# A running log-sum-exp: loads issued by GpSimd, stores by SyncE

## The chip, the cores and the metric

The kernel runs on one core of one Trainium2 chip. The metric is the device time of one execution in microseconds (us). Three runs of the kernel before gave 1262.72, 1262.72 and 1263.03 us, median 1262.72 us.

The core's engines are called PE (matrix products), ACT (ScalarE, exponentials and logarithms), DVE (VectorE), POOL (GpSimd) and SP (SyncE, which only issues transfers here). Transfers between DRAM and the on-chip memory are carried out by 16 DMA engines, whichever engine issues them.

## The reference

```python
B, S, D = (4, 4096, 4128)
out[:, 0, :] = x[:, 0, :].copy()
for t in range(1, S):
    mx = np.maximum(out[:, t - 1, :], x[:, t, :])
    out[:, t, :] = mx + np.log(np.exp(out[:, t - 1, :] - mx) + np.exp(x[:, t, :] - mx))
```

For each of the 4 batches and 4128 columns, row t of the output is the logarithm of the sum of the exponentials of rows 0 to t of the input. Input and output are fp32, 270.5 MB each.

## The kernel before

The work is cut into 44 *steps*. A step is a run of 384 rows of one batch (r = 3 rows for each of the 128 partitions), or 256 rows (r = 2) for one step in each batch: the first of batch 0, the last of the others. Partition p holds the r consecutive rows that begin at row p*r of the step, so its part of a transfer is one contiguous run of r x 4128 x 4 bytes: 49,536 bytes for r = 3, 33,024 for r = 2. A transfer of a step is 6192 KB or 4128 KB.

A step's tile `xt` is loaded once (line 127), worked on in place, and stored once from the same tile (line 130). The pool `xpool` has four such tiles, so step s uses the buffer of step s-4.

A step is worked in four *chunks* of columns: three of 1024 and a last one of 1056, whose last 32 columns (the tail) go through a small tile `qt`. For each chunk:

- `exp` (line 142): ACT takes the exponential of all r rows at once and writes fp16 over the tile's own memory.
- `head` (lines 92 and 96): PE sums over partitions with triangular fp16 matrices into a PSUM tile `pt`, and adds the carry of the step before, through the matrix `pick`.
- `stage(j)` for row j: ACT takes the logarithm of `pt` into the tile (line 175); PE then adds the next row through the identity. After the last row `keep` (lines 106 and 107) lets DVE save the last sums as the carry, split into two fp16 parts.

The order of the work is written out by hand in the loop of lines 205 to 218, and each engine carries out its instructions in that order. In turn g, ACT does the logarithms of chunks g-2, g-1 and g, then the exponential of chunk g+2. So the last logarithms of a step come after the first exponentials of the next step, and ACT stands still in the middle of a step's end when the next step's load has not landed.

Transfers: the first four loads are issued ahead of everything (lines 199 and 200). After a step's last logarithm its store is issued (line 211) and right behind it the load of the step three further on (line 213), into the buffer whose store was issued a step earlier. All loads and stores are issued by SP, in one queue. An instruction in a queue waits for its own conditions and holds up those behind it: a store waits for ACT's last logarithm of its step, a load for the landing of the store that last used its buffer.

POOL builds four constant matrices at the start (`_constants`, lines 18 to 46) and does nothing more; its last two instructions there are the two selects that make `pick`.

Of the kernel before, what the change touches and what calls it, by code (L numbers as in the profile page):

```python
# [49 lines left out]
def kernel(  # L50
# [11 lines left out]
    nc = tc.nc  # L62
# [49 lines left out]
    class Step:  # L112
# [10 lines left out]
        def load(self):  # L123
            full = xpool.tile([P, R, D], FP32, name="xt")
            self.xt = full[:, :self.r, :]
            self.half = self.xt.bitcast(FP16)
            nc.sync.dma_start(out=self.xt, in_=self.dram(x))  # L127

        def store(self):
            nc.sync.dma_start(out=self.dram(out), in_=self.xt)  # L130
# [118 lines left out]
```

## Time and profile before

| | |
|---|---|
| median of 3 runs | 1262.72 us |
| span of the profiled execution, first to last instruction | 1261.0 us |
| median of the runs less that span | 1.7 us |
| ACT busy | 947.0 us (75%) |
| PE busy | 690.7 us (55%) |
| DVE busy | 451.4 us (36%) |
| POOL busy | 2.2 us, 13 instructions |
| moved by DMA | 541.46 MB, 429 GB/s over the span |
| read from and written to HBM | 270.53 MB each |
| load of 6192 KB, issue to landing, median | 42.2 us |
| store of 6192 KB, issue to landing, median | 28.1 us |
| granted TensorE clock, mean | 0.779 |

The page gives no other time of the profiled execution than its span. The span begins with the first instruction and ends with the last; the median of the runs holds 1.7 us more.

"Busy" is the time in which an engine works on an instruction; issuing a transfer and waiting are not counted. A line "A <- B: total, times, longest" says that A sat idle until B released it. "SPq" is SP's queue of transfers. A transfer's line in the timeline gives the time at which it was issued and how long the issuing took, not the moving of the bytes. The trace also holds a record of each DMA packet, with start, duration and size.

### The profile page before, as it was taken

What the parts mean: (1) busy time and instruction counts of PE and PEld (TensorE: products, weight loads), DVE (VectorE), ACT (ScalarE), POOL (GpSimd) and SP (SyncE); (2) the same over time, 40 slices, a digit from 0 to 9 for tenths busy, and PEclk for the clock granted to TensorE, in tenths of its full rate; (3) what the DMA queues carried; (4) which work ended last, traced back from release to release, by engine and by line L of the source; (5) the groups of instructions that cost most, each with busy time, mean ns of one, the idle gap of its engine ahead of it and who ended that gap; (6) DMA issues with size and microseconds to landing.
All of it is one profiled execution on the core that took longest, in us unless ns stands there. A gap on an engine that the chain in (4) does not pass through costs nothing.

```text
span 1261.0 us, 6165 instructions
## 1 busy us (share of the span) xinstructions
PE 690.7 (55%) x2268; PEld 236.3 (19%) x2268; DVE 451.4 (36%) x445; ACT 947.0 (75%) x733; POOL 2.2 (0%) x13
## 2 busy tenths in 40 slices
PE   3666545565565555555346655555534755555562
PEld 1222111121121111111112221211211211111120
DVE  2443333333333333334424333333442433333344
ACT  5997777777777777778569777777866977777784
POOL 0000000000000000000000000000000000000000
PEclk9987787877777777878778777777777778787776
DMA  9999999999999999999999999999999999999998
GB/s 411 411 443 428 432 429 437 431 431 434 437 429 431 431 439 431 434 427 434 436 431 433 434 431 438 430 434 432 435 431 433 437 430 434 433 434 431 433 420 348
DMA packets 12702, 541.46 MB, mean 429 GB/s; under 512 B 1408, under 2 KB 1408, under 8 KB 1408
## 3 DMA queue, kind: packets, MB, share of 16 engines
q1 hardware_dynamic: 12672, 541.07, 99.4%
q8 instruction: 18, 0.29, 0.1%
q14 instruction: 12, 0.10, 0.0%
HBM read 270.53 MB, written 270.53 MB: 429 GB/s over the span
## 4 chain that ended last, share of the span: by engine, by line
DMA 72%; ACT 19%; PE 5%; issue 2%; DVE 1%; SPq 0%; ACTq 0%
DMA xt<-in_x_dram 67%; ACT xt L142 10%; ACT xt L175 9%; DMA out_dram<-xt 5%; PE pt L96 3%; PE pt L92 2%; DVE carry L106 0%; DVE carry L107 0%; ACT xt L180 0%; SPq L130 0%; ACTq L244 0%; SPq L127 0%; ACTq L142 0%; PE qt L92 0%
## 5 line engine op out<-in xcount | busy, mean ns | idle before, releaser
L142 ACT ACTIVATE xt<-xt 128x3072 f16<-128x3072 f32 (+3 forms) x176 | 478.2, 2717 | 247.9 <-DMA xt<-in_x_dram 247.8
L175 ACT ACTIVATE xt<-pt 128x1024 f32<-128x1024 f32 x512 | 487.3, 1029 | 2.5 <-PE pt L96 0.7
L106 DVE CAST carry<-pt 32x1024 f16<-32x1024 f32 x176 | 216.5, 1230 | 760.9 <-ACT xt L175 760.7
L92 PE MATMUL pt<-xt,ident 128*128 128x512 f16 x176 | 76.6, 435 | 493.7 <-ACT xt L175 493.7
L96 PE MATMUL pt<-xt,ident 128*128 128x512 f16 x496 | 203.7, 477 | 35.4 <-ACT xt L175 34.7
L107 DVE TENSOR_TENSOR carry<-pt,carry 32x1024 f16<-32x1024 f32 x176 | 215.8, 1226 | 6.1
L96 PE MATMUL pt<-xt,excl 128*128 128x512 f16 x496 | 187.6, 496 | 0.0
L96 PEld LDWEIGHTS <-ident 128*128 128x128 f16 x496 | 51.0, 103 | 655.0 <-issue 641.3
L92 PE MATMUL pt<-xt,incl 128*128 128x512 f16 x176 | 92.2, 524 | 23.5 <-ACT xt L142 15.1
L92 PE MATMUL pt<-xt,excl 128*128 128x512 f16 x176 | 93.4, 531 | 0.0
L96 PE MATMUL pt<-xt,incl 128*128 128x512 f16 x176 | 92.9, 528 | 0.0
L96 PEld LDWEIGHTS <-excl 128*128 128x128 f16 x536 | 66.6, 124 | 104.1 <-issue 79.5
L92 PE MATMUL pt<-carry,pick 128*128 128x512 f16 x160 | 72.0, 450 | 0.0
L96 PE MATMUL pt<-carry,pick 128*128 128x512 f16 x160 | 68.5, 428 | 0.0
L180 ACT ACTIVATE xt<-qt 128x96 f32<-128x96 f32 (+1 forms) x44 | 10.9, 248 | 46.3 <-PE pt L96 46.3
L92 PEld LDWEIGHTS <-incl 128*128 128x128 f16 x220 | 22.6, 103 | 118.0 <-DVE carry L107 95.3
L92 PEld LDWEIGHTS <-excl 128*128 128x128 f16 x220 | 26.8, 122 | 36.8 <-issue 27.9
L96 PEld LDWEIGHTS <-incl 128*128 128x128 f16 x260 | 27.8, 115 | 10.9 <-issue 4.8
L92 PEld LDWEIGHTS <-pick 128*128 128x128 f16 x200 | 22.9, 114 | 30.4 <-issue 20.4
L96 PEld LDWEIGHTS <-pick 128*128 128x128 f16 x160 | 18.4, 115 | 28.6 <-issue 17.2
L92 PEld LDWEIGHTS <-ident 128*128 128x128 f16 x176 | 19.2, 109 | 22.7 <-issue 12.8
L106 DVE CAST carry_t<-qt 32x32 f16<-32x32 f32 x44 | 8.7, 197 | 26.0 <-ACT xt L180 25.8
(21 smaller groups left out, 56.5 us busy)
## 6 DMA issues: line engine op xcount, KB each, us to landing
xt<-in_x_dram SPq DMA_DIRECT2D x40, 6192.0 KB, 42.2
out_dram<-xt SPq DMA_DIRECT2D x40, 6192.0 KB, 28.1
xt<-in_x_dram SPq DMA_DIRECT2D x4, 4128.0 KB, 37.3
out_dram<-xt SPq DMA_DIRECT2D x4, 4128.0 KB, 29.6
```

What stands on the lines that cost most here:

```text
L92: nc.tensor.matmul(pt, lhsT=w, rhs=rhs, start=start, stop=stop, skip_group_check=True)
L96: pe.add_instruction(mybir.InstMatmult(name=nc.get_next_instruction_name(), ins=[pe.lower_ap(rhs), pe.lower_ap(w, for_matmul_weights=True) ...
L106: nc.vector.tensor_copy(cr[HI:HI + 32, :], pt[HI:HI + 32])
L107: nc.vector.tensor_tensor(out=cr[LO:LO + 32, :], in0=pt[HI:HI + 32], in1=cr[HI:HI + 32, :], op=mybir.AluOpType.subtract,)
L142: nc.scalar.activation(self.t.half[:, :, 2 * c0:2 * c0 + w], self.t.xt[:, :, c0:c0 + w], ACT.Exp,)
L175: nc.scalar.activation(t.xt[:, j, c * CH:(c + 1) * CH], pt, ACT.Ln)
L180: nc.scalar.activation(t.xt[:, :, t0:D], self.qt, ACT.Ln)
```

## The change

The loads are issued by GpSimd, whose DMA descriptors are written by software; the stores stay on SP's hardware queue. One line differs:

```diff
         def load(self):
             full = xpool.tile([P, R, D], FP32, name="xt")
             self.xt = full[:, :self.r, :]
             self.half = self.xt.bitcast(FP16)
-            nc.sync.dma_start(out=self.xt, in_=self.dram(x))
+            nc.gpsimd.dma_start(out=self.xt, in_=self.dram(x))
 
         def store(self):
             nc.sync.dma_start(out=self.dram(out), in_=self.xt)
```

In the built program, the order of instructions on PE, DVE and ACT is the same as before. SP's list holds the 44 stores alone. POOL's list holds the 44 loads in the same order: the first stands between the two selects of `pick`, the others behind the second. Each of the 40 later loads carries its waits, the landing of a store among them, onto POOL.

## The prediction

> **What bounds the kernel now.** I read the page's DMA part first, because the engine part leaves it open: ACT, the busiest engine, works 75% of the span.
>
> ```profile
> DMA  9999999999999999999999999999999999999998
> q1 hardware_dynamic: 12672, 541.07, 99.4%
> DMA 72%; ACT 19%; PE 5%; issue 2%; DVE 1%; SPq 0%; ACTq 0%
> ```
>
> The first line is the share of the 16 DMA engines that is busy, in 40 slices; the second says that one queue (SP's) carried 12,672 packets and 541.07 MB and kept the engines busy for 99.4% of the span; the third is the chain that ended last. The kernel is bound by the DMA engines, not by a wait: 0.994 x 1261.0 = 1253.4 us of the span they are at work. Next, the table of stretches (columns: length, busy time of PE, PEld, DVE, ACT, POOL, granted clock, DMA share, GB/s):
>
> ```profile
> 0.00:15.00 15.00, 0.00 (x0) 0.10 (x1) 1.96 (x5) 3.15 (x2) 2.16 (x13) 1.00 0.94 387
> 100.00:1180.00 1080.00, 598.06 (x1953) 203.96 (x1953) 383.26 (x376) 815.74 (x631) 0.00 (x0) 0.77 1.00 433
> 1215.00:1230.00 15.00, 8.70 (x35) 3.12 (x34) 5.84 (x7) 12.53 (x12) 0.00 (x0) 0.89 0.93 401
> 1230.00:1245.00 15.00, 8.68 (x32) 2.92 (x31) 12.59 (x13) 12.79 (x13) 0.00 (x0) 0.89 0.79 338
> 1245.00:1261.00 16.00, 0.00 (x0) 0.00 (x0) 2.00 (x2) 0.00 (x0) 0.00 (x0) 0.51 0.84 363
> ```
>
> From 100 to 1180 us the share is 1.00 and the rate 433 GB/s; all the idle DMA time lies at the edges: 0.06 x 15 = 0.9 us at the start, and 1.05 + 3.15 + 2.56 = 6.8 us in the last 46 us. So anything that only moves waits in the middle is worth nothing; a change must alter the cost of a byte, the start, or the tail.
>
> The cost of a byte is in the trace's packet records: a packet of 33,024 B (a partition's part of a two-row step) takes 1222 ns, one of 49,536 B (three rows) 1829 ns, both medians, loads and stores alike. The difference, 607 ns for 16,512 B, is 27.2 GB/s for one engine, and leaves 1222 - 607 x 2 = 8 ns fixed for a packet. Only 3.9 us per engine is lost in packets that took longer than these medians.
>
> Last, who holds up the queue (waits of SP, then of ACT: total, times, longest):
>
> ```profile
> SPq L130 <- ACT xt L175: 1174.4, 44, 30.0
> SPq L127 <- DMA out_dram<-xt: 18.4, 5, 4.9
> ```
> ```profile
> ACT xt L142 <- DMA xt<-in_x_dram: 247.8, 42, 11.8
> ```
>
> SP stands nearly always at a store, waiting for the last logarithm. A load behind it found its buffer's earlier store already landed in all but 5 of its waits (18.4 us in all).
>
> **The change, part by part.** It removes 44 loads from SP's queue, adds 44 to POOL's, and so splits one ring of descriptors on each DMA engine into two, loads and stores. By the listing of both programs PE, DVE and ACT keep their order. Each load after the fourth now waits on POOL for its buffer's store to land; behind that wait stand only later loads, and who waits for those is ACT's first exponential.
>
> 1. *A load no longer stands behind the next store's wait for ACT.* Here is one period:
>
> ```profile
> 1153.19 0.33 SPq L130 DMA_DIRECT2D out_dram<-xt  x1
> 1153.61 0.38 SPq L127 DMA_DIRECT2D xt<-in_x_dram  x1
> 1182.54 0.33 SPq L130 DMA_DIRECT2D out_dram<-xt  x1
> 1182.97 0.38 SPq L127 DMA_DIRECT2D xt<-in_x_dram  x1
> ```
>
> The load follows the store by 0.43 us, once in 29.36 us, which is the engines' time for one load and one store: 2 x 8 x 1.829 = 29.3. The earlier store that frees the buffer takes 28.1 us (median, page) from issue to landing, so it lands about 1.2 us before. In two rings with equal turns a store of 14.6 us takes twice that, 29.3: the load is released where it was, within about 1 us. Value: 0. What hides an error is the work queued: a load lands 42.2 us after its issue, of which the store ahead and its own transfer are 29.3, so about 13 us of the load before is still running. With that cover gone ACT would wait longer, and as the engines would then run dry, each us would be one us of time.
>
> 2. *SP's issue time.* 44 x 0.383 us leaves SP; the engines had work meanwhile. 0.
>
> 3. *POOL's side.* Generating descriptors in software is not in this trace. Below: the 0.383 us that SP needs. Above: a row of unlike work, the 1.5 us of SP's longest load issue. Either is far below the 13 us of cover, so 0 in steady state. The Trainium skill speaks against the change here ("SBUF — State Buffer", Door 1's box on the "DVE blocks DMA" trap): a VectorE instruction in a two-port mode locks GpSimd out of the port it writes descriptors through. The trace has DVE at 451.4 us, its casts 1230 ns for 1024 elements a lane, from PSUM; I read 1.2 ns an element as no such mode. Were the rule to apply, a load would start at most one cast, 1.2 us, late each time, behind the 13 us: the sum would be the same.
>
> 4. *The start.* This is not hidden: the engines are saturated from the first packet on, so what the first load loses, the end loses. SP issues it at 0.80 us, and the packet records show its first data at 1.8 us. On POOL it comes between the two selects for `pick`:
>
> ```profile
> 1.95 0.29 POOL L35 TENSOR_SCALAR_AFFINE_SELECT ident<-ident 128x128 f16<-128x128 f16 x1
> 2.20 0.65 POOL L35 TENSOR_SCALAR_AFFINE_SELECT pick<-pick 128x128 f16<-128x128 f16 x2
> ```
>
> The first of the last pair ends at about 2.5: 1.7 us later than SP's 0.80. From issue to first data SP needs 1.0 us; on POOL the extra lies between 0 and three times SP's longest issue (dispatch, generation, start), 4.5 us. I take 1.3, as the usual rows (0.4 and 1.0) are nearer the low end. Together +3.0, from +1.7 to +6.2.
>
> 5. *The tail.* Before, the last load is issued at 1182.97 and lands at 1220.64; the last stores but one and two are issued at 1211.96 and 1234.00. By the packet records the engines ran dry before the store of 1234.00 for 3.4 us each in the mean. With two rings: at 1183 the load before the last has half its time, 7.3 us, left and lands 14.6 later, at 1197.6 (now 1196.1); the store issued with it lands at 1212; the last load (9.8 us) has had 7.3 by then and shares with the next store until 1217; that store's other 12.1 us end at 1229. ACT, from a landing at 1197.6, reaches the next store at about 1234 as before (it waited only 1.3 us for the last load). The hole is then 1229 to 1235, 6 us instead of 3.4: +2.6. The other end is that the hole closes: -3.4. I take +1.
>
> 6. *Cost of a load's bytes by software descriptors and of turns between rings.* 5,632 load packets on 16 engines are 352 for each. Below: the 3.9 us of stretched packets vanish if the other ring fills such gaps. Above: a load's 49,536 B are cut into their three rows, 2 x 8 ns x 352 = 5.6 us; into 4,096 B pieces, 12 x 8 ns x 352 = 33.8 us. I take 0: both kinds carry the same access shape, 128x12384, and that row is the nearest. The Trainium skill has a rule against it ("DMA: Bandwidth & Descriptors", Measured): its table for loads issued from GpSimd gives 79.0 us for 16 MB, which is 212 GB/s by its own two columns, though it prints 425 GB/s beside them; by the times, an estimate from that page, the loads alone would need 1274 us and the program far more than now, by the printed rate hardly more than now. No run here shows a software load yet; I side with the printed rate, since the row of 1829 ns stands for 433.
>
> **Sum:** span 1261.0 + 3.0 (start) + 0 (steady) + 1 (tail) + 0 (bytes) = 1265.0. The runs shown have a median of 1262.72, 1.7 above the profiled span; the forecast is 1265.0 + 1.7 = **1266.7 us**.
>
> **Rivals.** A measurement of this kernel tells about 0.2% from no change, 2.5 us: 1260.2 to 1265.2.
>
> - *Only the start and tail move* (forecast, 0.55): 1261 to 1272. For it: share 1.00 over 1080 us. About three fifths of it lies above 1265.2.
> - *The two rings fill the holes* (not slower; 0.18): a ring with loads gives an engine work while the other is empty or stretched, so the 3.4 us of the tail and the 3.9 us of long packets go, and the start keeps its least, +2: 1262.7 - 7.3 + 2 = 1257.4. It decides as soon as the start costs less than what is recovered. Against it: the hole at the tail is ACT's last step, which no ring shortens.
> - *Software descriptors or turns between rings cost* (slower by more; 0.25): 12.6 us, 1%, needs 36 ns for a load packet; pieces of 4 KB give 1262.7 + 33.8 + 3 = 1299.5, 50 ns give 1262.7 + 17.6 + 2.7 = 1283. It decides from 8 ns, where 2.8 us pass the bound. Against it: 8 ns fixed is all a packet costs now.
> - *The change is no change* (0.02): the loads wait for the same landings as before, POOL starts as early as SP; 1262.7.
>
> **The numbers.** Faster: the second case, 0.18. Same: two fifths of the first and the last, 0.22 + 0.02, less a little that I give to the slower side: 0.23. Slower: 0.59. The range goes from the second case's 1257.4 to the third's 1283 at 50 ns; I leave out some 0.05 below and 0.12 above.
>
> **What would show it.** Two dynamic queues with half the packets each, of the same sizes and durations (step 6); first load on POOL near 2.5 us, its data near 5 (step 4); loads still issued about every 29.3 us, stores landing in about 29 (step 1); 433 GB/s in the middle; the tail's share near that of now (step 5). I am wrong if the middle's rate falls below 430 or load packets multiply (third rival), if the last 46 us lose less than 4 us (second), or if POOL's issue takes over 13 us.

## The result, and the profile after

The changed kernel takes 1279.87 us, the median of four runs (1270.31 to 1284.79), against 1262.85 us for the kernel before (1262.72 to 1263.03). The ratio is 1.0125, 95% interval 1.0106 to 1.0144: slower by 1.25%. (In ratios, an execution over 1.5% above the quickest of its kernel is left out as slow; below there is one such, of 1287.70 us.) Not only the level has changed: the runs of before lie within 0.3 us, those after within 14.5 us. The profiled execution is the quickest of the four, 1270.31 us with a span of 1268.6 us. It shows where 7.6 us went; a second trace, further down, shows a slower execution, of 1276.32 us. No execution as slow as the median was traced.

The page's DMA queues and chain of the changed kernel:

```profile
DMA packets 12703, 541.47 MB, mean 427 GB/s; under 512 B 1408, under 2 KB 1408, under 8 KB 1408
q0 software_dynamic: 6336, 270.54, 49.7%
q1 hardware_dynamic: 6336, 270.54, 49.5%
...
DMA 65%; ACT 27%; issue 4%; PE 3%; DVE 0%; POOL 0%; ACTq 0%; POOLq 0%
```

Two queues carry half each, with as many packets as before, and by the packet records the software queue's packets have the same sizes and the same medians, 1222 and 1829 ns. So the packets of the software queue are not smaller, and a packet's usual cost is the same. The engines are still busy for 99.2% of a longer span. The stretches of the changed kernel (same columns as in the prediction: the last two are DMA share and GB/s):

```profile
0.00:15.00 15.00, 0.00 (x0) 0.00 (x0) 1.97 (x5) 1.28 (x1) 4.38 (x17) 1.00 0.81 328
100.00:550.00 450.00, 248.88 (x801) 84.80 (x801) 153.23 (x150) 335.14 (x257) 7.95 (x15) 0.75 1.00 433
580.00:620.00 40.00, 26.98 (x88) 9.31 (x88) 22.24 (x22) 36.59 (x32) 0.53 (x1) 0.80 0.96 399
880.00:920.00 40.00, 22.99 (x81) 8.03 (x80) 14.56 (x14) 30.94 (x25) 1.06 (x2) 0.79 1.01 426
```

The same two short stretches of the kernel before:

```profile
580.00:620.00 40.00, 22.67 (x82) 7.81 (x81) 18.92 (x18) 29.43 (x25) 0.00 (x0) 0.84 1.01 435
880.00:920.00 40.00, 23.05 (x80) 7.90 (x79) 15.52 (x16) 34.24 (x29) 0.00 (x0) 0.80 1.00 433
```

The start has less of its first 15 us (share 0.81 against 0.94). From 100 to 550 us nothing is lost. Two new losses appear, and they look different: from 580 to 620 us the share falls to 0.96, engines stand idle; from 880 to 920 us the share is 1.01 and the rate still only 426 GB/s: engines are "busy", but with packets that take longer. (A packet's whole time counts in the stretch in which it starts, so a share can pass 1.00.) Both stretches lie around a two-row step.

The loads' waits on POOL, the page's issue lines for the three-row steps, and the issue times around the first hole, of loads and then of a store, in the changed kernel:

```profile
POOL xt L127 <- ACT xt L175: 742.8, 26, 29.0
POOL xt L127 <- DMA out_dram<-xt: 347.9, 11, 65.1
```
```profile
xt<-in_x_dram POOLq DMA_DIRECT2D x40, 6192.0 KB, 36.2
out_dram<-xt SPq DMA_DIRECT2D x40, 6192.0 KB, 35.6
```
```profile
567.49 0.53 POOL L127 DMA_DIRECT2D xt<-in_x_dram  x1 [29.26 <-ACT xt L142]
592.82 0.53 POOL L127 DMA_DIRECT2D xt<-in_x_dram  x1 [24.80 <-ACT xt L175]
624.31 0.53 POOL L127 DMA_DIRECT2D xt<-in_x_dram  x1 [30.96 <-DMA out_dram<-xt]
```
```profile
592.52 0.33 SPq L130 DMA_DIRECT2D out_dram<-xt  x1
```

Each load now waits on POOL, and what it waits for is a landing: where the profile names ACT it infers, since by the listing the conditions are the same each time, the landing and earlier work of ACT that the store itself had waited for. The median load lands 36.2 us after its issue (42.2 before), the median store 35.6 (28.1 before). With equal turns a transfer of 14.64 us needs 29.3 us, so 6.9 us of a load's time and 6.3 of a store's are left for what comes ahead of its own packets. One ring had 13 us of work ahead of a load; each of the two has about half that time in hand. (That 6.9 and 6.3 add up to 13 proves nothing: the two rings run side by side, so these are waits and not amounts of work.) As the store that frees a buffer lands later, the load is issued later too: 6.8 us behind the store that was issued last (median of 40), where it was 0.4 us. At the hole, SP issued a store at 592.52, POOL a load at 592.82. By the packet records most engines had ended all earlier work of both rings by 591 to 593 and got the new store's first packet at 593.4, the new load's at 598 to 600, 5 to 7 us after its issue; the store's packet just before the load's took 2.4 to 3.0 us instead of 1.83 on nearly all engines. So there is first an idle time, as both rings are empty, and then a stretched packet. The fine stretches show the idle time, first in the profiled execution, then, at the same place, in the second trace of the same kernel:

```profile
590.00:592.00 2.00, 2.00 (x6) 0.76 (x5) 0.00 (x0) 2.00 (x2) 0.00 (x0) 0.50 0.73 314
```
```profile
592.00:594.00 2.00, 2.00 (x7) 0.75 (x5) 0.00 (x0) 2.00 (x2) 0.00 (x0) 0.51 0.16 66
```

**A ledger.** The packet records allow a full account of a span: the time to the first data, 1249.6 us per engine for all packets at their medians (1248.8 for 10,240 packets at 1829 ns and 1024 at 1222 ns, divided by 16, and 0.8 for 1408 semaphore packets at 9 ns), what packets took beyond these medians ("stretched"), idle engine time between first and last packet ("gaps"), and what follows the last packet. The last column counts first packets of a transfer that started on an engine whose ring for that kind of transfer had had nothing for over 2 us; two-ring kernels only.

| us per engine | span | first data | stretched | gaps | after the last | ring dry at start |
|---|---|---|---|---|---|---|
| before | 1261.0 | 1.8 | 4.4 | 3.9 | 1.3 | - |
| changed | 1268.6 | 3.9 | 8.0 | 5.6 | 1.5 | 26% |
| changed, second trace | 1274.6 | 4.0 | 10.8 | 8.8 | 1.5 | 49% |

The 7.6 us of the profiled execution are 2.1 (start) + 3.6 (stretched) + 1.7 (gaps, of which 0.3 in the last 60 us) + 0.2. In the second trace, of 1276.32 us, the start is the same, and stretched packets and gaps take 6.4 and 4.9 us. So in these two traces the start is fixed, and the difference between them lies in the other two.

### The profile page after: what moved, and what is told of

It is laid out like the page before. It is cut to its first block, busy times and chain, and to the rows that moved or that the text cites. A ratio compares the mean times of both kernels' runs of the same rounds, so it can differ in the third digit from the quotient of the medians.

```text
span 1268.6 us, 6172 instructions
## 1 busy us (share of the span) xinstructions
PE 688.0 (54%) x2268; PEld 236.8 (19%) x2268; DVE 451.4 (36%) x445; ACT 947.3 (75%) x733; POOL 25.6 (2%) x57
## 2 busy tenths in 40 slices
DMA packets 12703, 541.47 MB, mean 427 GB/s; under 512 B 1408, under 2 KB 1408, under 8 KB 1408
## 4 chain that ended last, share of the span: by engine, by line
DMA 65%; ACT 27%; issue 4%; PE 3%; DVE 0%; POOL 0%; ACTq 0%; POOLq 0%
DMA xt<-in_x_dram 51%; DMA out_dram<-xt 14%; ACT xt L142 14%; ACT xt L175 13%; PE pt L96 2%; PE pt L92 1%; ACT xt L180 0%; DVE carry L106 0%; DVE carry L107 0%; ACTq L244 0%; POOL xt L127 0%; POOL pick L35 0%; POOL ident L35 0%; POOL excl L25 0%; POOLq L127 0%
## 5 line engine op out<-in xcount | busy, mean ns | idle before, releaser
L92 PE MATMUL pt<-xt,incl 128*128 128x512 f16 x176 | 91.7, 521 | 26.3 <-ACT xt L142 17.4
L127 POOL DMA_DIRECT2D xt<-in_x_dram x44 | 23.5, 533 | 1173.0 <-ACT xt L175 742.8
L92 PEld LDWEIGHTS <-pick 128*128 128x128 f16 x200 | 22.6, 113 | 29.7 <-issue 19.3
## 6 DMA issues: line engine op xcount, KB each, us to landing
xt<-in_x_dram POOLq DMA_DIRECT2D x40, 6192.0 KB, 36.2
out_dram<-xt SPq DMA_DIRECT2D x40, 6192.0 KB, 35.6
```

What stands on the lines that cost most here:

```text
L92: nc.tensor.matmul(pt, lhsT=w, rhs=rhs, start=start, stop=stop, skip_group_check=True)
L127: nc.gpsimd.dma_start(out=self.xt, in_=self.dram(x))
```

## The experiments

Times are medians with lowest and highest and the number of runs; "before" beside them was 1262.78, 1262.91 and 1262.88 us in the three groups, within 0.6 us of its median each time.

### First group: software descriptors, or two rings?

Theory A blamed two rings, theory B the software descriptors.

**Two hardware rings.** ACT issues the stores.

```diff
-            nc.sync.dma_start(out=self.dram(out), in_=self.xt)
+            nc.scalar.dma_start(out=self.dram(out), in_=self.xt)
```

> Loads stay on SP's hardware queue, the stores are issued by ACT's hardware queue: two rings, but no software descriptors. Theory A (two rings whose loads and stores run at the same time stretch packets, wherever the descriptors come from): 1270 to 1285 us, with a spread of some us between executions, as in the changed kernel, less its late start of 2.5 us. Theory B (the software descriptors cost): 1262 to 1266 us with the small spread of before, the difference being ACT's issue of 44 stores.

Measured: 1265.30 us (1264.83 to 1277.23, 8 runs), ratio 1.0047 (1.0018 to 1.0077). Neither theory has it right. Five runs lie at 1264.8 to 1265.3, one at 1267.6, two at 1276.4 and 1277.2: two rings alone can cost 14 us, without a single software descriptor, but mostly don't. The trace is of a quick execution (1265.01 us); the slow ones have none.

**One software ring.** GpSimd issues loads and stores, in the order of before.

```diff
-            nc.sync.dma_start(out=self.xt, in_=self.dram(x))
+            nc.gpsimd.dma_start(out=self.xt, in_=self.dram(x))
-            nc.sync.dma_start(out=self.dram(out), in_=self.xt)
+            nc.gpsimd.dma_start(out=self.dram(out), in_=self.xt)
```

> Loads and stores are all issued by GpSimd, in the order that SP had before: software descriptors, but one ring. Theory A: the start is 2.5 us later, all else as before: 1264 to 1267 us, small spread. Theory B: at least as slow as the changed kernel, 1275 us or more, as twice as many descriptors are written by software.

Measured: 1268.34 us (1268.24 to 1268.39, 4 runs), ratio 1.0043 (1.0028 to 1.0058). Theory B, with its 1275 us or more, falls. The page and its issue lines:

```profile
q0 software_dynamic: 12672, 541.07, 99.0%
...
xt<-in_x_dram POOLq DMA_DIRECT2D x40, 6192.0 KB, 41.8
out_dram<-xt POOLq DMA_DIRECT2D x40, 6192.0 KB, 27.8
```

With all 88 transfers in software the times to landing are those of before, and so is the spread. In the ledger the 5.5 us of span are 2.2 at the start, 3.8 after the last packet (5.1 against 1.3), +0.5 stretched, -0.9 gaps: nothing in the body. The end, which puts the time above theory A's 1267 us, was not expected: POOL's longest drain at the end took 19.4 us, while the last packet ended at 1261.4.

**Loads on SP, stores on GpSimd.**

```diff
-            nc.sync.dma_start(out=self.dram(out), in_=self.xt)
+            nc.gpsimd.dma_start(out=self.dram(out), in_=self.xt)
```

> Loads on SP, stores on GpSimd: two rings, the software one carrying the stores, and the start as early as before. Theory A: 1268 to 1283 us, the changed kernel's time less 2.5 us of start, with its spread. Theory B, with a cost for each software descriptor: about the same as the changed kernel, 1270 to 1283 us; with a cost that lies in the reading side of the software ring alone, 1262 to 1266 us.

Measured: 1268.11 us (1265.98 to 1275.73, 8 runs), ratio 1.0052 (1.0031 to 1.0073). Two rings again, and again a spread: four runs near 1266.3, the others from 1269.7 to 1275.7. Of the profiled execution's 3.4 us, 1.7 lie after the last packet. The median does not tell theory B's variants apart; the spread is theory A's.

**The changed kernel again**, with no edit.

> The changed kernel unchanged, on the chip of the other three, for a second trace and for its spread. Both theories: 1270 to 1285 us. If the spread comes from packets that are stretched, as 7.8 us per engine of the first trace against 3.9 before, the trace of a slower execution has correspondingly more of it; if it comes from gaps between packets, the DMA share in the middle falls below 1.00.

Measured: 1278.90 us (1268.03 to 1287.70, 5 runs), ratio 1.0107 (1.0067 to 1.0147) for the four up to 1282.51 us, whose median is 1277.61. The stretches of its trace:

```profile
100.00:550.00 450.00, 245.54 (x809) 83.69 (x808) 153.23 (x150) 332.89 (x256) 7.95 (x15) 0.76 1.00 433
580.00:620.00 40.00, 26.18 (x82) 8.74 (x82) 20.04 (x20) 37.57 (x32) 0.53 (x1) 0.76 0.93 386
880.00:920.00 40.00, 23.66 (x80) 8.16 (x79) 15.13 (x14) 32.87 (x26) 1.06 (x2) 0.80 0.97 403
```

The same places as in the first trace, and both dips deeper: 0.93 and 0.97 in the share. Both answers of the expectation hold together, more stretched packets and lower shares.

What follows: the loss needs two rings, and where it was traced it comes with empty rings. Empty rings alone do not set its size: in the traces of the two other kernels with two rings, both of quick executions, the packet records find about a fifth of the first packets on a dry ring, hardly fewer than the quarter in the first trace of the changed kernel, and no more than 1.4 us of stretched packets and 1.1 us of gaps beyond the kernel before. The loss was seen around the two-row steps, so the next theory (C) was that these short steps empty the rings; its rival (D), that a software load ring beside a store ring stretches packets anywhere.

### Second group: the short steps

**Two-row steps only, six buffers of the same bytes in all, on SP.** 64 equal steps.

```diff
-R = 3
+R = 2
...
-    bufs = 4
+    bufs = 6
```

> All steps have two rows (64 equal steps, six buffers of the same bytes in all), loads and stores on SP: the baseline for the next run. The bytes are the same, the tail shorter by a third of a step: 1255 to 1263 us, small spread, in both theories.

Measured: 1264.15 us (1263.97 to 1264.58, 10 runs), ratio 1.0011 (1.0001 to 1.0020); a little above the expected range.

**The same with the change's line**, loads on GpSimd.

> The same 64 equal steps, loads on GpSimd. Theory C (two rings lose only where a short step leaves the load ring without queued work, as a load is released by a store that now lands later): 2 to 4 us above the run with SP's loads, which is the later start, and a spread under 2 us. Theory D (a software load ring beside a store ring stretches packets anywhere): 8 to 20 us above it, with a spread of some 10 us.

Measured: 1267.14 us (1267.03 to 1267.65, 6 runs), 3.0 us above SP's, within 0.6 us. Theory D falls: two rings, one of them software, 128 transfers, and nothing is lost in the middle. One stretch and the issue lines:

```profile
100.00:1100.00 1000.00, 517.61 (x1807) 194.85 (x1807) 521.04 (x510) 773.15 (x663) 26.84 (x51) 0.79 1.00 433
```
```profile
xt<-in_x_dram POOLq DMA_DIRECT2D x64, 4128.0 KB, 51.0
out_dram<-xt SPq DMA_DIRECT2D x64, 4128.0 KB, 38.9
```

Share 1.00 and 433 GB/s for 1000 us. A transfer of 9.78 us needs 19.6 with equal turns, so a load has 31 us queued before it and a store 19: each ring holds about a whole transfer or more in stock. Only 3% of the transfers' first packets found a dry ring, and 3.3 us are stretched, less than in the kernel before.

**The short steps left out, on SP**, and then with loads on GpSimd. 256 rows of each batch stay unwritten.

```diff
-        parts = [R] * (n // R) + ([n % R] if n % R else [])
+        parts = [R] * (n // R)
```

> Left out: the two-row step of each batch, 256 of its 4096 rows, which stay unwritten; 40 equal steps of three rows, four buffers, all on SP. 78 us less transfer time than before: 1181 to 1187 us, small spread, in both theories. It is the baseline for the next run.

> The changed kernel with the same 256 rows of each batch left out: 40 equal steps of three rows, loads on GpSimd. Theory C (the loss comes at the two-row steps): 2 to 5 us above the same kernel with SP's loads, spread under 3 us. Theory D: 8 to 18 us above it, with a spread of some 10 us.

Measured: 1188.91 us on SP (1188.48 to 1189.75, 4 runs), 1209.32 us with loads on GpSimd (1193.47 to 1211.14, 4 runs). The 20.4 us between them are more than in the full kernel, with no short step left: theory C falls too. First SP's kernel, then GpSimd's:

```profile
700.00:880.00 180.00, 102.59 (x331) 34.91 (x331) 64.06 (x64) 135.96 (x107) 0.00 (x0) 0.76 1.00 433
```
```profile
100.00:550.00 450.00, 244.82 (x808) 83.91 (x807) 154.20 (x151) 333.71 (x257) 7.92 (x15) 0.76 1.00 431
700.00:880.00 180.00, 98.73 (x324) 33.52 (x324) 61.29 (x60) 132.02 (x102) 3.51 (x7) 0.76 1.00 422
```

With loads on GpSimd the share is 1.00 and the rate falls from 431 to 422 as the execution goes on (433 on SP): here a "busy" DMA engine is not one at full rate. In the ledger the 20.8 us of span are 2.1 (start), 13.3 (stretched: 17.5 against 4.2), 5.3 (gaps, nearly all in the last 60 us, where step 5's hole is); 73% of the first packets found a dry ring. Half of the stretch, 8.8 us, is in the first packets of stores that did.

The two pairs agree in one thing: what differs between no loss and 20 us is how much is queued in each ring. That is theory E, and it can be tried with the size of a step held.

### Third group: what is queued

**Two-row steps, four buffers, on SP**, and then with loads on GpSimd: the kernels of the second group's first pair without the edit of `bufs`.

```diff
-R = 3
+R = 2
```

> 64 equal two-row steps, but four buffers instead of six, all on SP: the baseline for the next run. In one ring a transfer follows another without a gap as long as something is queued: 1262 to 1270 us in both theories, small spread.

> The same with the loads on GpSimd. Theory E (what costs is that a ring runs dry and starts again, because each load is released by a landing store and too few buffers leave nothing queued): 6 to 25 us above the same kernel with SP's loads, spread of 3 us or more. Theory F (steps of 33 KB for a partition don't suffer, steps of 49.5 KB do): 2 to 4 us above it, spread under 1 us, as with six buffers.

Measured: 1269.16 us on SP (1267.86 to 1269.48, 4 runs), 1279.46 us with loads on GpSimd (1278.05 to 1283.76, 4 runs): 10.3 us apart, where six buffers gave 3.0. The issue lines of GpSimd's kernel:

```profile
xt<-in_x_dram POOLq DMA_DIRECT2D x64, 4128.0 KB, 26.3
out_dram<-xt SPq DMA_DIRECT2D x64, 4128.0 KB, 24.0
```

Less the 19.6 us that a transfer needs in turns, 6.7 us are left for a load and 4.4 for a store. Little of this is queued work, since 81% of the first packets found a dry ring. Most of it is the restart: where an engine's ring was empty at a load's issue, the first packet came 5.2 us after the issue (median), at a store's issue 3.0 us, though the other ring's packets take 1.2 us each. With nothing else under way it is about 1 us: 0.9 for SP's last stores, 1.4 for GpSimd's first load. Of the 9.0 us between the two spans 2.1 are the start, 4.8 stretched packets and 2.0 gaps.

**Five buffers, loads on GpSimd.** `R = 2`, `bufs = 5`.

> Two-row steps, five buffers, loads on GpSimd. Theory E: between the runs with four and with six buffers, nearer to six, as one more step is queued: 1266 to 1272 us. Theory F: 1267 us as with six.

Measured: 1267.12 us (1266.98 to 1267.61, 6 runs), as with six. Its issue lines:

```profile
xt<-in_x_dram POOLq DMA_DIRECT2D x64, 4128.0 KB, 31.4
out_dram<-xt SPq DMA_DIRECT2D x64, 4128.0 KB, 38.9
```

Less 19.6 us that is 11.8 us before a load and 19.3 before a store; 6% of the first packets found a dry ring, and 3.2 us are stretched. One buffer of 33 KB a partition is worth 12.3 us here, and a second one nothing. Theory F falls, as the step's size is the same in all of these. (With all loads on SP, five buffers were not run.)

**Six buffers, the first six loads on SP.**

```diff
-        def load(self):
+        def load(self, q=nc.gpsimd):
...
-            nc.gpsimd.dma_start(out=self.xt, in_=self.dram(x))
+            q.dma_start(out=self.xt, in_=self.dram(x))
...
-        s.load()
+        s.load(nc.sync)
```

> Two-row steps, six buffers, the first six loads issued by SP, the other 58 by GpSimd: the start alone is undone. If the 3.0 us by which six buffers with GpSimd's loads stand above SP's are the later start (first data at 3.9 us instead of 1.8), this gives 1264.5 to 1265.5 us; if they are a cost of every load, it stays at 1267.

Measured: 1265.35 us (1264.83 to 1272.86, 10 runs). The median is 1.8 us lower; first data comes at 1.8 us instead of 3.9, and nothing else in the ledger moves by more than 0.2. The 1.2 us that are left above SP's kernel are gaps, all in the last 60 us (6.6 us against 5.3). So of the 3.0 us about two are the start and the rest is the end. Two of ten runs, at 1272.3 and 1272.9, have no trace and no explanation here.

None of the kernels that write all rows is quicker than the kernel before.

## Why the prediction was right, and where not

The direction and the range (1257.4 to 1283) held; the likeliest case, 1266.7, did not: 1279.9 lies 13 us above it and outside its 1261 to 1272. It is near what the third rival gave for 50 ns a packet, but by another mechanism, so that the range held was luck. The term of the sum that failed is the 0 for the steady part: beyond the start and the last 60 us, stretched packets and gaps cost 5.0 us in the first trace and 10.5 in the second. Two of the signs that the prediction named failed as well: stores landed after 35.6 us and not 29, and the rate from 100 to 1180 us was 431 GB/s in the first trace and 429 in the second, with 430 as the bound.

- **Step 1 failed**, in its value 0 and in what was to hide an error: "a load lands 42.2 us after its issue, of which the store ahead and its own transfer are 29.3, so about 13 us of the load before is still running". In two rings 6.9 us were left ahead of a load and 6.3 ahead of a store. A store lands after 35.6 us, not 29.3, and so the load was not "released where it was, within about 1 us", but 6.8 us behind a store instead of 0.4. The rings ran dry at 26% and 49% of the transfers' first packets in the two traces. The runs with two-row steps show that this is what costs, as only the number of buffers differs: with four, 81% dry, the kernel takes 10.3 us more than with all loads on SP; with six, 3% dry, 3.0 us more, which are the start and the end; and with five, 6% dry, it takes as long as with six. The changed kernel itself was not run with more buffers. The sentence that time is lost when the cover is gone was right; that a packet also takes longer when rings run dry, and that a dry ring takes some 5 us to start again beside a busy one, was in no step.
- **Step 2 and step 3** held. POOL's issue takes 0.53 us, SP's took 0.383, which is small beside 6.9 us of cover as well as beside 13. With all 88 transfers on POOL beside the same DVE work the body lost nothing. The rule that was weighed there (the Trainium skill, "SBUF — State Buffer", SBUF: two separate sides, the "DVE blocks DMA" trap) is neither confirmed nor refuted: the casts here take 1.2 ns an element, which the prediction read as no such mode, and no run has casts of another speed beside a software load.
- **Step 4**: right in kind, +2.1 instead of +3.0. The first load is issued where it was expected, and its data comes 1.4 us later, against SP's 1.0: +0.4 where 1.3 was taken. The idle 0.9 us that the prediction read off the DMA share of the first 15 us were 2.0 us by the packet records; the sum does not use them. The lines of the changed kernel:

```profile
2.21 0.29 POOL L35 TENSOR_SCALAR_AFFINE_SELECT pick<-pick 128x128 f16<-128x128 f16 x1
2.56 0.67 POOL L127 DMA_DIRECT2D xt<-in_x_dram  x1
```

- **Step 5**: the gaps of the last 60 us are 5.1 us against 4.8 in the first trace: +0.3 where +1 was taken.
- **Step 6**: right for software descriptors, whose packets are the same to the ns; the one software ring has 0.5 us more stretch than before. Of the table in the Trainium skill ("DMA: Bandwidth & Descriptors", Measured) the printed rate fits and the time column does not: 1829 ns for 49,536 B on each of 16 engines is 433 GB/s, also in software. For turns between rings the value 0 holds only while both are stocked; the loss is not a price per packet, as step 6 and the third rival had it.
- The second rival, two rings that fill each other's holes, has a little in its favour: with five or six buffers of two rows 3.2 and 3.3 us are stretched, against 3.9 in one ring with the same steps. These 0.6 to 0.7 us are less than the start costs.

**What stays open.** Why a packet is stretched when a ring starts dry was not settled: without the short steps half of the stretch sat in the first packets of stores on dry rings; in the run with four two-row buffers those first packets had 0.5 of 9.1 us. Nor was it settled why an empty ring beside a busy one needs so long to start again. It is open, too, why GpSimd's loads fall into the lossy course more often than SP's, whose two rings have about as little in hand (5.0 and 7.9 us with ACT's stores, 5.3 and 6.7 with GpSimd's): of the changed kernel's eight runs up to 1284.79 us six took over 1275 us, of the sixteen with SP's loads and stores elsewhere three. Where the ring was empty, GpSimd's loads started 5.2 to 5.8 us after their issue (medians of four traces), SP's 4.2 to 4.5 (two traces). That this microsecond makes the difference is not shown; no run isolated it.

## What to carry to other kernels

Splitting loads and stores over two queues splits the time in hand too. Count for each ring the time to landing less a transfer's own time in turns: in these runs time was lost, in some executions or in all, where that was a third of the transfer's time in turns or less; where it was 0.6 or more, nothing beyond start and end in 20 of 22 executions. In between nothing was measured. The wait that the change took off the queue was worth nothing here, as the DMA engines were saturated, and its cover had to be computed in the new order, not read from the old. Read the DMA share together with GB/s, since stretched packets count as busy, and take several executions when their times spread.

## What the runs showed of the hardware that was not expected

- With work in both rings each DMA engine alternates, one packet of a load, one of a store, for packets of 49,536 B as of 33,024 B: of those packets that directly follow another big one, over 99% are of the other kind. This agrees with the Trainium skill ("DMA: Bandwidth & Descriptors", Queues, rings and completion order), which has engines take turns between queues at packet granularity.
- An empty ring starts late beside a busy one: with four two-row buffers a load's first packet came 5.2 us after its issue and a store's 3.0 us, where one packet of the other ring takes 1.2 us.
- The same program took 1268 to 1285 us from one execution to the next when its rings ran dry, while two of the three kernels with stocked rings, and the one with a single software ring, stayed within 0.7 us.
- Stores on the software ring prolonged the end: 3.0 us (stores alone) and 5.1 us (loads and stores) from the last packet to the last instruction instead of 1.3, with a drain on POOL of 17.4 and 19.4 us.
